# A channel shuffle: loads and stores moved from two DMA queues to one, with 4 MB tiles in place of 2 MB and all copies on VectorE

## The chip, the cores and the metric

The kernel runs on one core of one Trainium2 chip. The metric is the device time of one execution in microseconds, and lower is better. "Span" is the profiled part of an execution.

## The reference

The input is a float32 array of 16 x 64 x 64 pixels with 256 channels, 67.11 MB. The channels of each pixel are seen as 8 groups of 32, and the two axes are swapped.

```python
def reference(x, groups):                      # x: (16, 64, 64, 256), groups: 8
    batch, h, w, c = x.shape
    x = x.reshape(batch, h, w, groups, c // groups)
    x = x.transpose(0, 1, 2, 4, 3)
    return x.reshape(batch, h, w, c).astype(np.float32)
```

There is no arithmetic. Every byte is read once from HBM, moved within its pixel, and written once: 134.22 MB in all.

## The kernel before

Each tile gives each of the 128 partitions 16 whole pixels, 16 KB, which lie together in DRAM. A tile is loaded from SyncE, permuted by one strided copy on GpSimd or VectorE in turn, and stored from ScalarE. Loads and stores therefore stand in two DMA queues, and five buffers on each side let them run ahead.

```python
q = 16                                   # pixels per partition: 16 KB rows, 2 MB tiles, 32 tiles
in_pool = ...tile_pool(name="in_pool", bufs=5)
out_pool = ...tile_pool(name="out_pool", bufs=5)
copy_engines = [nc.gpsimd, nc.vector]
for t in range(ntiles):
    in_tile = in_pool.tile([P, free], mybir.dt.float32)
    nc.sync.dma_start(out=in_tile, in_=x_t[t])
    out_tile = out_pool.tile([P, free], mybir.dt.float32)
    src = in_tile.rearrange("p (i g j) -> p i j g", g=G, j=CPG)
    dst = out_tile.rearrange("p (i j g) -> p i j g", j=CPG, g=G)
    copy_engines[t % 2].tensor_copy(out=dst, in_=src)
    nc.scalar.dma_start(out=out_t[t], in_=out_tile)
# [... views, asserts and the launch are cut ...]
```

Of the kernel before, what the change touches and what calls it, by code (L numbers as in the profile page):

```python
# [2 lines left out]

# [4 lines left out]


_Q = int(os.environ.get("CS_Q", "16"))
_IN_BUFS = int(os.environ.get("CS_IN_BUFS", "5"))
_OUT_BUFS = int(os.environ.get("CS_OUT_BUFS", "5"))
_COPY_ENGINES = os.environ.get("CS_COPY_ENGINES", "gv")


@with_exitstack
def kernel(
    ctx: ExitStack,
    tc: tile.TileContext,  # L20
    x: bass.AP,
    groups: bass.AP,
    out: bass.AP,
):
    nc = tc.nc

    b, h, w, c = x.shape
    G = int(groups)
    CPG = c // G
    assert G * CPG == c, (c, G)  # L30

    P = nc.NUM_PARTITIONS

    n_pix = b * h * w
    assert n_pix % P == 0

    q = _Q
    pix_per_tile = P * q
    ntiles = n_pix // pix_per_tile
    assert ntiles * pix_per_tile == n_pix, (n_pix, pix_per_tile)  # L40

    free = q * c

    x_t = x.rearrange("b h w c -> (b h w c)").rearrange(
        "(t p f) -> t p f", p=P, f=free
    )
    out_t = out.rearrange("b h w c -> (b h w c)").rearrange(
        "(t p f) -> t p f", p=P, f=free
    )

    in_pool = ctx.enter_context(tc.tile_pool(name="in_pool", bufs=_IN_BUFS))
    out_pool = ctx.enter_context(tc.tile_pool(name="out_pool", bufs=_OUT_BUFS))

    eng_map = {"v": nc.vector, "g": nc.gpsimd, "s": nc.scalar}
    copy_engines = [eng_map[ch] for ch in _COPY_ENGINES]

    def do_copy(eng, dst, src):
        if eng is nc.scalar:
            eng.copy(out=dst, in_=src)
        else:  # L60
            eng.tensor_copy(out=dst, in_=src)  # L61

    for t in range(ntiles):
        in_tile = in_pool.tile([P, free], mybir.dt.float32)
        nc.sync.dma_start(out=in_tile, in_=x_t[t])  # L65

        out_tile = out_pool.tile([P, free], mybir.dt.float32)

        src = in_tile.rearrange("p (i g j) -> p i j g", g=G, j=CPG)
        dst = out_tile.rearrange("p (i j g) -> p i j g", j=CPG, g=G)  # L70
        do_copy(copy_engines[t % len(copy_engines)], dst, src)

        nc.scalar.dma_start(out=out_t[t], in_=out_tile)


# [1 line left out]
_INS = ['x', 'groups']  # L77
_OUTS = [((16, 64, 64, 256), 'float32')]
#: Inputs that are plain numbers.
_NUMBERS = {'groups': 8}  # L80


# [26 lines left out]
```

## Time and profile before

| | before |
|---|---|
| time, median | 317.98 us (317.81 to 318.05, 4 runs) |
| span | 316.3 us |
| DMA queues | 2, together 99.5% of the 16 engines' span |
| VectorE / GpSimd busy | 63.8 us / 114.7 us |
| one 16 KB packet, steady part | 611 ns |

The first lines are from the profile page of the kernel before: busy tenths of VectorE (DVE), GpSimd (POOL) and the DMA engines in 40 equal slices of the span, what the DMA moved in each slice, and the queues.

```profile
DVE  0344004040130402204021040310404004040040
POOL 0863350803508044080530806217062260713500
DMA  7999999999999999999999999999999999999997
GB/s 290 431 402 431 431 431 431 431 431 433 431 431 431 431 431 431 431 431 431 431 431 431 431 431 431 431 431 431 431 431 431 431 431 431 431 431 431 433 431 332
...
q1 hardware_dynamic: 4608, 67.11, 50.0%
q10 hardware_dynamic: 4608, 67.11, 49.5%
```

The DMA engines are full from end to end and the copy engines are idle most of the time. This kernel is bound by its transfers.

The next view, windows of the kernel before, gives for chosen stretches (start:end in us) the length, the busy time of VectorE and GpSimd with the number of instructions, the clock, the DMA engines' busy share and GB/s.

```profile
4.00:8.00 4.00, 0.00 (x0) 0.00 (x0) 1.00 1.01 434
16.00:20.00 4.00, 3.19 (x1) 1.68 (x1) 1.00 1.01 381
20.00:24.00 4.00, 0.00 (x0) 4.00 (x1) 1.00 1.00 410
40.00:80.00 40.00, 7.70 (x2) 15.22 (x3) 1.00 1.01 431
304.00:308.00 4.00, 0.00 (x0) 0.00 (x0) 1.00 1.01 434
312.00:314.00 2.00, 0.00 (x0) 0.00 (x0) 1.00 1.03 442
314.00:316.00 2.00, 0.00 (x0) 0.00 (x0) 1.00 0.21 90
316.00:318.00 2.00, 0.00 (x0) 0.00 (x0) 1.00 0.00 0
```

Loads alone (4 to 8 us), loads and stores mixed (40 to 80) and stores alone (304 to 308) run at the same 431 to 434 GB/s. There is one dip where the stores begin.

From the page again: the groups of copies (count, then busy time and mean ns of one, then idle time before them and what ended it), and the DMA issues (count, size, median time from issue to landing).

```profile
L61 POOL COPY out_tile<-in_tile 128x4096 f32<-128x4096 f32 x16 | 114.5, 7157 | 182.3 <-DMA in_tile<-in_x_dram 182.3
L61 DVE COPY out_tile<-in_tile 128x4096 f32<-128x4096 f32 x16 | 63.8, 3985 | 240.0 <-DMA in_tile<-in_x_dram 240.0
...
in_tile<-in_x_dram SPq DMA_DIRECT2D x32, 2048.0 KB, 38.8
out_dram<-out_tile ACTq DMA_DIRECT2D x32, 2048.0 KB, 25.3
```

### The profile page before, as it was taken

Reading aid. Unit: us, or ns where it says so; the run is one execution under the profiler, and the core shown is the slowest. Engines: PE = TensorE matmul, PEld = TensorE weight load, DVE = VectorE, ACT = ScalarE, POOL = GpSimd, SP = SyncE. Lnnn points to the kernel's source line nnn. Section 1 sums busy time; section 2 is a strip of 40 time slices with the busy share of each in tenths; the row PEclk is TensorE's granted clock in tenths of the full one; section 3 lists DMA queues with packets and bytes.
Section 4 is the critical chain, followed back from the end, with each engine's and each line's share of the span. In section 5 each row is a group of like instructions: output and inputs, shape, how many; then the busy total and the mean of one; then the engine's idle time right before and its main releaser. Section 6 shows DMA issues by size and latency. Waiting matters only on the chain.

```text
span 316.3 us, 247 instructions
## 1 busy us (share of the span) xinstructions
DVE 63.8 (20%) x16; POOL 114.7 (36%) x20
## 2 busy tenths in 40 slices
DVE  0344004040130402204021040310404004040040
POOL 0863350803508044080530806217062260713500
DMA  7999999999999999999999999999999999999997
GB/s 290 431 402 431 431 431 431 431 431 433 431 431 431 431 431 431 431 431 431 431 431 431 431 431 431 431 431 431 431 431 431 431 431 431 431 431 431 433 431 332
DMA packets 9216, 134.22 MB, mean 424 GB/s; under 512 B 1024, under 2 KB 1024, under 8 KB 1024
## 3 DMA queue, kind: packets, MB, share of 16 engines
q1 hardware_dynamic: 4608, 67.11, 50.0%
q10 hardware_dynamic: 4608, 67.11, 49.5%
HBM read 67.11 MB, written 67.11 MB: 424 GB/s over the span
## 4 chain that ended last, share of the span: by engine, by line
DMA 94%; DVE 1%; SPq 0%; issue 0%; DVEq 0%
DMA in_tile<-in_x_dram 94%; DVE out_tile L61 1%; SPq L65 0%; DVEq L61 0%
## 5 line engine op out<-in xcount | busy, mean ns | idle before, releaser
L61 POOL COPY out_tile<-in_tile 128x4096 f32<-128x4096 f32 x16 | 114.5, 7157 | 182.3 <-DMA in_tile<-in_x_dram 182.3
L61 DVE COPY out_tile<-in_tile 128x4096 f32<-128x4096 f32 x16 | 63.8, 3985 | 240.0 <-DMA in_tile<-in_x_dram 240.0
L90 POOL MEMSET const-float32-0.0<- 128x1 f32 x1 | 0.1, 99 | 0.2 <-issue 0.2
L90 POOL MEMSET const-bfloat16-1.0<- 128x1 bf16 x1 | 0.1, 103 | 0.0
L90 POOL MEMSET const-uint8-127<- 128x1 uint8 x1 | 0.1, 103 | 0.0
L90 POOL MEMSET const-float32-1.0<- 128x1 f32 x1 | 0.1, 99 | 0.0
## 6 DMA issues: line engine op xcount, KB each, us to landing
in_tile<-in_x_dram SPq DMA_DIRECT2D x32, 2048.0 KB, 38.8
out_dram<-out_tile ACTq DMA_DIRECT2D x32, 2048.0 KB, 25.3
```

What stands on the lines that cost most here:

```text
L61: eng.tensor_copy(out=dst, in_=src)
L90: nc = _bacc.Bacc("TRN2", target_bir_lowering=False, num_devices=1)
```

## The change

The change takes tiles of twice the size (32 KB per partition, 4 MB, 16 tiles), three buffers on each side, and all copies on VectorE in two halves per tile. SyncE issues everything. Three loads go first, and then store t and load t+3 alternate. The intent is fewer, larger transfers, and one queue in which the order of reads and writes is fixed.

```diff
-_Q = 16, _IN_BUFS = 5, _OUT_BUFS = 5, _COPY_ENGINES = "gv"     [four lines, shortened]
+_Q = 32
+_COPY = 16
+_BUFS = 3
 [...]
+    def load(t):
+        in_tile = in_pool.tile([P, _Q * c], F32, name="in_tile")
+        nc.sync.dma_start(out=in_tile, in_=x_t[t])
+        in_tiles[t] = in_tile
-    for t in range(ntiles):
-        in_tile = in_pool.tile([P, free], mybir.dt.float32)
-        nc.sync.dma_start(out=in_tile, in_=x_t[t])
-        [... one copy on GpSimd or VectorE ...]
-        nc.scalar.dma_start(out=out_t[t], in_=out_tile)
+    for t in range(_BUFS):
+        load(t)
+    for t in range(n_tiles):
+        in_tile = in_tiles.pop(t)
+        out_tile = out_pool.tile([P, _Q * c], F32, name="out_tile")
+        for k in range(0, _Q, _COPY):
+            [... src, dst: 16 pixels of the tile ...]
+            nc.vector.tensor_copy(out=dst, in_=src)
+        nc.sync.dma_start(out=out_t[t], in_=out_tile)
+        if t + _BUFS < n_tiles:
+            load(t + _BUFS)
```

More of the change, by code (lines that the diff above doesn't have):

```diff
@@ L2 @@
-import os
 from contextlib import ExitStack
@@ L8 @@
 from concourse._compat import with_exitstack
-_Q = int(os.environ.get("CS_Q", "16"))
-_IN_BUFS = int(os.environ.get("CS_IN_BUFS", "5"))
-_OUT_BUFS = int(os.environ.get("CS_OUT_BUFS", "5"))
-_COPY_ENGINES = os.environ.get("CS_COPY_ENGINES", "gv")
+F32 = mybir.dt.float32
+P = 128
+_Q = 32
+_COPY = 16
+_BUFS = 3
 @with_exitstack
@@ L29 @@
     CPG = c // G
-    assert G * CPG == c, (c, G)
-    P = nc.NUM_PARTITIONS
+    assert G * CPG == c
     n_pix = b * h * w
-    assert n_pix % P == 0
-    q = _Q
-    pix_per_tile = P * q
-    ntiles = n_pix // pix_per_tile
-    assert ntiles * pix_per_tile == n_pix, (n_pix, pix_per_tile)
-    free = q * c
+    n_tiles = n_pix // (P * _Q)
+    assert n_tiles * P * _Q == n_pix
     x_t = x.rearrange("b h w c -> (b h w c)").rearrange(
-        "(t p f) -> t p f", p=P, f=free
+        "(t p f) -> t p f", p=P, f=_Q * c
@@ L46 @@
     )
     out_t = out.rearrange("b h w c -> (b h w c)").rearrange(
-        "(t p f) -> t p f", p=P, f=free
+        "(t p f) -> t p f", p=P, f=_Q * c
     )
-    in_pool = ctx.enter_context(tc.tile_pool(name="in_pool", bufs=_IN_BUFS))
-    out_pool = ctx.enter_context(tc.tile_pool(name="out_pool", bufs=_OUT_BUFS))
-    eng_map = {"v": nc.vector, "g": nc.gpsimd, "s": nc.scalar}
-    copy_engines = [eng_map[ch] for ch in _COPY_ENGINES]
-    def do_copy(eng, dst, src):
-        if eng is nc.scalar:
-            eng.copy(out=dst, in_=src)
-        else:
-            eng.tensor_copy(out=dst, in_=src)
@@ L63 @@
-    for t in range(ntiles):
-        in_tile = in_pool.tile([P, free], mybir.dt.float32)
-        nc.sync.dma_start(out=in_tile, in_=x_t[t])
-        out_tile = out_pool.tile([P, free], mybir.dt.float32)
-        src = in_tile.rearrange("p (i g j) -> p i j g", g=G, j=CPG)
-        dst = out_tile.rearrange("p (i j g) -> p i j g", j=CPG, g=G)
-        do_copy(copy_engines[t % len(copy_engines)], dst, src)
-        nc.scalar.dma_start(out=out_t[t], in_=out_tile)
+    in_pool = ctx.enter_context(tc.tile_pool(name="in_pool", bufs=_BUFS))
@@ new lines @@
+    out_pool = ctx.enter_context(tc.tile_pool(name="out_pool", bufs=_BUFS))
+    in_tiles = {}
+    def load(t):
+        in_tile = in_pool.tile([P, _Q * c], F32, name="in_tile")
+        nc.sync.dma_start(out=in_tile, in_=x_t[t])
+        in_tiles[t] = in_tile
[5 more added lines that the diff above has]
+        for k in range(0, _Q, _COPY):
+            cols = slice(k * c, (k + _COPY) * c)
+            src = in_tile[:, cols].rearrange("p (i g j) -> p i j g", g=G, j=CPG)
+            dst = out_tile[:, cols].rearrange("p (i j g) -> p i j g", j=CPG, g=G)
+            nc.vector.tensor_copy(out=dst, in_=src)
+        nc.sync.dma_start(out=out_t[t], in_=out_tile)
+        if t + _BUFS < n_tiles:
+            load(t + _BUFS)
```

## The prediction

> **What bounds the kernel now.** The 16 DMA engines. The queue table gives 50.0% + 49.5% of their span, and the chain of waits is 94% input load. The windows view gives 434 GB/s at 4-8 us (loads alone), 431 at 40-80 us (both mixed) and 434 at 304-308 us (stores alone), so the rate depends neither on direction nor on the number of queues in use. In the packet records every 16 KB packet of the steady part takes 611 ns: 8192 packets / 16 engines x 0.611 us = 312.8 us of the 316.3 us span. The rest is the start (about 2.7 us until data flows), a dip when the first stores begin (windows view, 16-24 us: 381 and 410 GB/s, about 0.6 us lost), and the last completions. The Trainium skill, "DMA: Bandwidth & Descriptors", section "Where 436 GB/s comes from", states a ceiling of 435.2 GB/s; this trace reaches 431, 99% of it. VectorE is busy 63.8 us (20%), GpSimd 114.7 us (36%).
>
> **What the change removes.** All 16 GpSimd copies (7.11 us each) and ScalarE's store issues. VectorE takes everything: 32 copies of the same 128x4096 shape at 3.86 us (one that overlapped GpSimd took 5.79) = 124 us, 39% of the span, still hidden. DMA issues fall from 64 to 32, each 328-338 ns, off the critical path after the start. The 1024 completion packets of 9 ns become 512: 0.58 us per engine becomes 0.29.
>
> **What it moves.** Stores now stand in the same queue as loads: L0 L1 L2 S0 L3 S1 L4 ... Does the queue run dry? A 4 MB transfer takes about 9.7 us. L0 lands near 12 us, two copies end near 20, S0 and L3 are issued, while L1 and L2 keep the engines busy until about 31 us. In the steady state, when load t lands, S(t-2), L(t+1), S(t-1), L(t+2) are queued behind it: 39 us of work; S(t) follows after 7.8 us. So SyncE's waits have some 31 us of slack. At the end S13 and S14 (19 us) cover the last copy, so the tail stays one completion. The same page, section "Issuing engines are not separate DMA queues", says that queues of different issuers share the 16 engines, so giving up the second queue should cost no bandwidth; the trace agrees as far as it can (434 GB/s with one queue alone).
>
> **What may gain.** A row per partition grows from 16 to 32 KB. If it goes as one packet and part of the 611 ns is fixed per packet (estimate from the 435.2 GB/s ceiling: 16 KB would take 602 ns, so up to 9 ns), the transfer falls by up to 2.2 us. If it is cut into 16 KB packets, or has no fixed part, only about 0.3 us. I take a middle.
>
> **Predicted time.** 317.0 us, range 315.0 to 319.0. Chances: faster by over 2% 0.02, within 2% 0.93, slower by over 2% 0.05.
>
> **What would show it.** Right: 430-434 GB/s in every middle slice; one DMA queue; VectorE about 124 us over 32 copies; load issue to landing grows, because up to 20 MB queue ahead; the chain still DMA. Packets of 32 KB at 1214-1222 ns, or 16 KB at 611.
>
> **What would make it wrong.** The trace never shows one queue switching between loads and stores. If each of about 29 switches lost as much as the first stores' dip (0.6 us), that would be 17 us, 5% slower, visible as middle slices near 405 GB/s with longer packets. A limit on transfers outstanding in one queue would show as gaps between packets.

## The result, and the profile after

The changed kernel takes 321.07 us (320.31 to 321.86, 4 runs) against 317.98 us. The ratio is 1.0096, with a 95% interval of 1.0079 to 1.0113. Ratios here are the mean time of one kernel's fast runs over that of the other's of the same rounds, so they are not quite the ratio of the medians quoted. The change is slower by about 1%, and the time lies outside the predicted range of 315 to 319 us.

The profile page of the changed kernel, the same lines as shown of before:

```profile
DVE  0378813509045090440904408054080631707200
POOL 0000000000000000000000000000000000000000
DMA  8999999999999999999999999999999999999993
GB/s 328 431 423 394 431 423 443 414 447 431 431 431 423 443 431 423 439 419 435 435 431 431 414 447 431 427 435 419 443 439 419 439 410 456 431 419 439 419 451 135
...
q1 hardware_dynamic: 4608, 134.22, 98.2%
```

The DMA engines are still full, and one queue carries everything. The middle slices now scatter between 394 and 456 GB/s, where the prediction wanted 430 to 434 in each, but they average about the same. The last slice stands out: 135 GB/s where it was 332, with the DMA engines at 3 tenths where they had 7.

Windows of the changed kernel, with the same columns:

```profile
4.00:8.00 4.00, 0.00 (x0) 0.00 (x0) 1.00 0.95 410
28.00:30.00 2.00, 2.00 (x1) 0.00 (x0) 1.00 0.97 393
30.00:32.00 2.00, 0.34 (x1) 0.00 (x0) 1.00 1.03 262
40.00:80.00 40.00, 16.02 (x5) 0.00 (x0) 1.00 1.00 432
304.00:308.00 4.00, 0.00 (x0) 0.00 (x0) 1.00 0.95 410
312.00:314.00 2.00, 0.00 (x0) 0.00 (x0) 1.00 0.69 295
314.00:316.00 2.00, 0.00 (x0) 0.00 (x0) 1.00 0.30 131
316.00:318.00 2.00, 0.00 (x0) 0.00 (x0) 1.00 0.11 49
```

At 40 to 80 us the rate is 432 GB/s, no lower than before. From 312 us on it fades to 295, 131 and 49 GB/s over some six microseconds, where the kernel before stopped within two. The work is not slower on the whole: the 16 engines no longer finish together.

The group of copies and the DMA issues of the changed kernel, from its page:

```profile
L60 DVE COPY out_tile<-in_tile 128x4096 f32<-128x4096 f32 x32 | 122.4, 3880 | 175.0 <-DMA in_tile<-in_x_dram 175.0
...
in_tile<-in_x_dram SPq DMA_DIRECT2D x16, 4096.0 KB, 50.9
out_dram<-out_tile SPq DMA_DIRECT2D x16, 4096.0 KB, 41.2
```

VectorE does all 32 copies in 122.4 us and idles 175.0 us waiting for loads, so compute is still hidden. SyncE, however, waits for VectorE. The view of waits of the changed kernel, for the DMA queue's own sequencer (total us, times, longest):

```profile
SPq L61 <- DVE out_tile L60: 282.3, 16, 19.5
```

Those 282.3 us look alarming and cost nothing that shows. The DMA engines have 4 MB transfers queued meanwhile, and no slice between the first and the last falls below 9 tenths. (Run w2, below, takes away nearly all of this wait and is no faster.) A wait counts only if the engine that bounds the kernel runs dry.

**Where the engines part.** The Trainium skill, "DMA: Bandwidth & Descriptors", section "Why a DMA increments its semaphore by 16 and not by 1", says that a DMA over 128 partitions is split over 16 engines, each of which adds one to the semaphore when its part has landed. The trace agrees: it holds 1024 such increments for the 64 DMAs of before, and 512 for the 32 of after. The time from the first to the last of a DMA's 16 increments therefore tells how far the engines have drifted apart. I worked it out from the completion records of each trace. The columns are points at eighths of the DMAs, in order of completion, and the values are us:

```
                          1/8  2/8  3/8  4/8  5/8  6/8  7/8  last
before                    1.8  1.8  1.8  1.8  1.8  1.8  1.8  0.7
changed kernel            0.5  0.7  1.5  2.6  3.3  4.3  4.8  5.1
changed, again (d0)       0.5  0.7  1.2  2.9  3.3  4.4  5.0  5.2
```

In the kernel before, the engines keep a fixed distance and end 0.7 us apart. In the changed kernel, a few engines fall back steadily. At the end the last increment comes 4.6 us after the median one, and the first only 0.5 us before it. Every DMA has one increment from each engine, so the slowest engine sets when it is done, and the last DMA's slowest engine sets the time. No trace here shows an engine doing more than its share to help a late one.

**When they fall back.** The packet records show 32 KB packets of 1213 ns nearly throughout. After 40 us, 78 of the 4096 packets take over 1240 ns, up to 1872. Engines are not named in these records, so packets were chained to engines by their end and start times, with each engine held to 32 DMAs of 8 packets and one completion. Packets that end together can still be swapped. By this order, 76 of the 78 are among the last two packets that an engine does of a load before it turns to a store (78 of 90 in d0, and 50 of 53 in w2, below). Those places hold two of the 16 packets of a load and a store. The extra time is uneven: after 40 us four engines collect 3.4 to 4.1 us of it, two 1.2 and 1.5 us, and the other ten 0.3 us at most.

### The profile page after: what moved, and what is told of

Its sections match the earlier page's. It is cut to its first block, busy times and chain, and to the rows that moved or that the text cites. A ratio compares the mean times of both kernels' runs of the same rounds, so it can differ in the third digit from the quotient of the medians.

```text
span 319.4 us, 133 instructions
## 1 busy us (share of the span) xinstructions
DVE 122.4 (38%) x32; POOL 0.2 (0%) x4
## 4 chain that ended last, share of the span: by engine, by line
another core or an unknown queue 41%; DVE 30%; DMA 20%; DVEq 1%; issue 0%; SPq 0%
DVE out_tile L60 30%; DMA in_tile<-in_x_dram 20%; DVEq L94 1%; DVEq L60 0%; SPq L48 0%; SPq L61 0%
## 5 line engine op out<-in xcount | busy, mean ns | idle before, releaser
L60 DVE COPY out_tile<-in_tile 128x4096 f32<-128x4096 f32 x32 | 122.4, 3880 | 175.0 <-DMA in_tile<-in_x_dram 175.0
## 6 DMA issues: line engine op xcount, KB each, us to landing
in_tile<-in_x_dram SPq DMA_DIRECT2D x16, 4096.0 KB, 50.9
```

The lines of the kernel that those rows point to most:

```text
L60: nc.vector.tensor_copy(out=dst, in_=src)
```

## The experiments

I call a change from a load to a store in one queue's order a turn. The changed kernel has 14 of them (the last two stores follow a store). Theory A: turns in one queue make the engines fall apart, and the larger packets give back a part. Rival B: the 32 KB packets themselves share unevenly. Rival C: late issue, the buffers or VectorE.

All runs gave right results unless said otherwise. They were made in four sittings, each on a chip of its own: e1, e2, e3 and e4; c1, c2, c3 and e3b; the d runs; the w runs. The kernel before took 317.94 to 318.12 us (medians) beside them, so times of two sittings can be compared to about 0.2 us. Diffs are against the changed kernel unless said otherwise.

| run | queues | packets | turns | time, us | ratio to before (95%) | last spread, us |
|---|---|---|---|---|---|---|
| changed kernel | 1 | 32 KB | 14 | 321.07 | 1.0096 (1.0079 to 1.0113) | 5.1 |
| e1 | 2 | 32 KB | - | 323.73 | 1.0178 (1.0163 to 1.0193) | 1.8 |
| e2 | 1 | 16 KB | 27 | 320.91 | 1.0091 (1.0074 to 1.0108) | 3.4 |
| e3 | 1 | 32 KB | 6 | 318.19 | 1.0008 (0.9993 to 1.0023) | 0.6 |
| e4 | 2 | 32 KB | both turn | 324.63 | 1.0216 (1.0178 to 1.0255) | 7.0 |
| c1 | 2 | 16 KB | - | 317.87 | 1.0005 (0.9989 to 1.0021) | 1.3 |
| c2 | 1 | 16 KB | 14 | 321.75 | 1.0114 (1.0099 to 1.0130) | 4.6 |
| c3 | 2 | 16 KB | - | 317.72 | 0.9992 (0.9977 to 1.0007) | 0.4 |
| e3b | 1 | 32 KB | 6 | 319.95 | 1.0062 (1.0045 to 1.0079) | 0.6 |
| d0 (changed, again) | 1 | 32 KB | 14 | 321.39 | 1.0097 (1.0083 to 1.0112) | 5.2 |
| d1 | 1 | 8 KB | 53 | 321.85 | 1.0124 (1.0111 to 1.0137) | 1.8 |
| d2 | 2 | 32 load, 16 store | - | 327.95 (fast runs) | 1.0309 (1.0259 to 1.0359) | 4.9 |
| d3 | 2 | 16 load, 32 store | - | 323.72 | 1.0180 (1.0166 to 1.0193) | 0.2 |
| w1 (wrong result) | 1 | 32 KB | 1 | 316.12 | 0.9941 (0.9927 to 0.9954) | 0.7 |
| w2 (wrong result) | 1 | 32 KB | 14 | 321.25 | 1.0110 (1.0091 to 1.0129) | 4.5 |
| w4 | 1 | 32 KB | 4 | 317.27 | 0.9981 (0.9968 to 0.9994) | 1.2 |

Turns are counted from the order of issue. Two texts below give 29 turns for e2 and 61 for d1; with their six and twelve loads ahead, 27 and 53 are right. The last spread does not tell all: in e1 and d3 the engines part by up to 5.5 and 9.2 us before the end.

### e1: a queue of its own for the stores

```diff
-        nc.sync.dma_start(out=out_t[t], in_=out_tile)
+        nc.scalar.dma_start(out=out_t[t], in_=out_tile)
```

> Only edit against the changed kernel: the stores are issued from ScalarE, so they have a queue of their own; 4 MB tiles, 32 KB packets, three buffers and VectorE copies stay. Theory A (one queue turning from loads to stores costs: packets in flight at each turn are lengthened, unevenly over the engines): beyond the first stores nothing turns any more, so packets over 1240 ns are gone after the first stores' dip, the engines finish within 1 us of each other, and the 2.3 us from the larger packets are kept: 315 to 316.5 us, faster than both kernels (ratio to before 0.992 to 0.996). Rival B (32 KB packets themselves jitter and share unevenly over the engines): 320 to 322 us, still a long tail.

Measured: 323.73 us, a clear miss. With two queues the kernel became slower still. Beyond the first stores, load packets are lengthened about every 20 us, the duration of a 4 MB load and a 4 MB store side by side. Turns inside one queue cannot be the whole story, and 32 KB packets on two queues have a loss of their own. A part of it is waiting at the end: the last store was issued at 308.62 us, after its copies, and from 306.6 to 309.5 us the engines stood idle for 1.4 us on average. The changed kernel has no such gap.

### e2: 2 MB tiles on one queue

```diff
-_Q = 32
+_Q = 16
-_BUFS = 3
+_BUFS = 6
```

> One queue as in the changed kernel, but tiles of 2 MB in six buffers each (same SBUF, same order of loads and stores): 29 turns from loads to stores instead of 14, 16 KB packets of 611 ns as before. Theory A, with a fixed loss per turn: about 5.5 us lost (the changed kernel lost about 3 us to the before kernel and gave back 2.3) become about 10: 323 to 330 us, long packets at every turn. Rival B (packet size): with 16 KB packets back to 318 us. Rival C (single queue loses at its issue waits or at its end only): 320 to 322 us.

Measured: 320.91 us. The loss did not double, against A with a fixed loss per turn, and did not vanish with 16 KB packets, against B. It lies in the range of rival C, which w2 tests below. The spread grows to 3.4 us within the first third and then stays there: 1.0, 2.6, 3.5, 3.4, 3.4, 3.5, 3.5, 3.4 at the eighths. The lag thus stopped growing, here at about 70% of the 4.9 us that one DMA takes (8 packets of 611 ns).

### e3: loads and stores in groups of three

The order in the queue becomes three loads, three stores, and so on (3, 3, 3, 3, 2, 2 tiles).

```diff
-    for t in range(_BUFS):
-        load(t)
-    for t in range(n_tiles):
-        [... copy t, store t ...]
-        if t + _BUFS < n_tiles:
-            load(t + _BUFS)
+    first = 0
+    for size in [3, 3, 3, 3, 2, 2]:
+        these = range(first, first + size)
+        first += size
+        for t in these:
+            load(t)
+        for t in these:
+            copy(t)              # the same two copies, then the store
```

> One queue, 4 MB tiles, but the order is three loads, three stores (3,3,3,3,2,2 tiles): 6 turns from loads to stores instead of 14; everything else as in the changed kernel. The queue should not run dry: with groups of two and more the copies end while other transfers are queued. Theory A: loss shrinks to 5 of 13 turns after the first: 316.5 to 318.5 us. Rival B (packet size): 320 to 322 us, as the changed kernel.

Measured: 318.19 us, as A expected. The spread never exceeds 1 us, and the engines end together. One thing was not foreseen: at 274 us, where a store is followed by a load, all 16 engines lost about 0.9 us at once.

### e4: two queues that turn in opposed phases

```diff
+    queues = [nc.sync, nc.scalar]
-        nc.sync.dma_start(out=in_tile, in_=x_t[t])
+        queues[t % 2].dma_start(out=in_tile, in_=x_t[t])
-        nc.sync.dma_start(out=out_t[t], in_=out_tile)
+        queues[t % 2].dma_start(out=out_t[t], in_=out_tile)
```

> Two queues, but each turns: even tiles load and store on SyncE's queue, odd tiles on ScalarE's, so that each queue turns 6 or 7 times, in opposed phases (while one loads the other stores) and the sum of loads and stores in flight stays mixed. If the turn costs in the queue (A1, each ring pays when it goes from a load to a store): long packets at the turns, loss as with one queue, 319 to 322 us. If it costs because the whole flow turns from reading HBM to writing it (A2): no long packets after the first stores, 315 to 317 us.

Measured: 324.63 us, outside both ranges, with a spread that grows to 7.0 us. The test decides nothing between A1 and A2. Its 32 KB packets stand on two queues, where e1 lost time without any turns in a queue, and the flow was not evenly mixed: in the packet records, 11 or more of the 16 engines were on the same queue at three moments of four, for instance 14 on one queue at 103.0 us and 14 on the other 1.2 us later.

### c1: e2 with two queues

```diff
# against e2
-        nc.sync.dma_start(out=out_t[t], in_=out_tile)
+        nc.scalar.dma_start(out=out_t[t], in_=out_tile)
```

> The kernel e2 (2 MB tiles, six buffers each, VectorE copies) with its stores on ScalarE's queue: one edit from e2, and from the kernel before it differs only in six buffers for five and in VectorE for both copy engines. If the one queue costs what e2 lost: 317.5 to 318.3 us, all engines' completions within 2 us of each other to the end. If VectorE alone or the buffer count were at fault: 320 to 322 us.

Measured: 317.87 us. One word moves the time from 320.91 to 317.87 us. The two ran on different chips, but the kernel before took 317.94 and 318.00 us beside them; c2 and c3 repeat the pair on one chip. VectorE alone and six buffers change nothing against the kernel before, so that part of rival C is out. One queue costs 3.0 us at 2 MB.

### c2: the changed kernel with 16 KB packets

```diff
     x_t = x.rearrange("b h w c -> (b h w c)").rearrange(
-        "(t p f) -> t p f", p=P, f=_Q * c
+        "(t k p f) -> t p k f", k=2, p=P, f=_Q * c // 2
     )                                        # out_t likewise
-        nc.sync.dma_start(out=in_tile, in_=x_t[t])
+        nc.sync.dma_start(out=in_tile.rearrange("p (k f) -> p k f", k=2), in_=x_t[t])
                                              # the store likewise
```

> The changed kernel with the same 4 MB DMAs in the same order, but each partition's row cut into two DRAM pieces of 16 KB, so packets of 16 KB (611 ns expected). If stragglers come from the order of the DMAs (turns of 4 MB in one queue): the spread of the engines' completions still grows to about 5 us, and time is the changed kernel's plus 2.3 us of packet cost, 322 to 324.5 us. If they come from 32 KB packets: the spread stays under 2 us and time is 317.5 to 319.5 us.

Measured: 321.75 us, and the spread grows to 4.6 us (0.7, 1.2, 2.2, 2.7, 3.0, 3.4, 4.1, 4.6). The stragglers do not come from 32 KB packets: rival B is out for one queue. The time is a little under the range given; the drift is a little smaller too.

### c3: e1 with 16 KB packets

This is c2 with its stores on ScalarE.

> The kernel e1 (two queues, 4 MB DMAs, three buffers, 323.7 us) with packets of 16 KB. If e1's loss came from 32 KB packets taking turns on two queues: 317.5 to 319 us. If it came from DMAs of 4 MB with three buffers: 323 to 326 us, the spread growing to about 5 us as in e1.

Measured: 317.72 us, with the spread constant at 1.6 us and 0.4 at the end. The DMA engines' busy tenths, first c2 (one queue), then c3 (two queues):

```profile
DMA  7999999999999999999999999999999999999993
```

```profile
DMA  7999999999999999999999999999999999999997
```

The same DMAs of 4 MB with three buffers are as fast as the kernel before, as soon as the packets are 16 KB. The loss of e1 belongs to 32 KB packets on two queues.

### e3b: other groups

```diff
# against e3 (shortened to the list of groups)
-[3, 3, 3, 3, 2, 2]
+[3, 2, 3, 3, 3, 2]
```

> As e3 (one queue, grouped loads and stores) but groups of 3,2,3,3,3,2 tiles, to see whether e3's second stall of all engines (0.9 us at 274 us, after two pairs in a row) comes again and where. If it belongs to pairs or to the end: a stall after the first pair or near the end, 318 us. If it was chance: one stall only, at the first stores, 316.5 to 317.5 us. The spread of completions should stay under 1.5 us.

Measured: 319.95 us, well over what either case expected. The engines stay within 2.1 us (1.5 was expected) and end 0.6 us apart, but stalls of all engines came at about 100 and 130 us, after the first pair, beside the one at the first stores. The first of the two came at the end of the pair, where a store is followed by a load, just as in e3; the second came one turn later. That speaks for pairs and against chance, but why pairs should do it no run shows. Few turns keep the engines nearer together, but they do not guard against this second loss. The 0.6 us at the end flatters, for the queue also ran dry: the first store of the last pair was issued only at 295.97 us, after its copies, and from 295.5 to 296.9 us up to eleven of the 16 engines stood idle. That let the late ones catch up, so the lag they had by then was lost time all the same.

### d0: the changed kernel again

> The changed kernel again, unedited, beside the next three on one chip: 320.3 to 322 us, and the spread of the engines' completions of one DMA again growing from about 0.6 us to 4 to 6 us. If the spread were an accident of one profile, it would stay under 2 us.

Measured: 321.39 us, with the spread growing to 5.2 us as in the first profile. The drift is a property of the kernel and not of one profile.

### d1: 1 MB tiles on one queue

```diff
-_Q = 32, _COPY = 16, _BUFS = 3
+_Q = 8, _COPY = 8, _BUFS = 12
```

> One queue in the same order, tiles of 1 MB (8 KB packets), twelve buffers each: 61 turns, but only 2.4 us of loads between turns. With 602 ns per 16 KB and 9 ns per packet fixed, as 611 and 1213 ns say, an 8 KB packet takes 310 ns and the transfer grows by 4.6 us over 16 KB packets. Stragglers: in e2 (2 MB) the spread stopped growing at 3.4 us, 70% of one DMA; if a straggler can lag no more than part of one DMA, it stops near 1.7 us here: 322.5 to 325 us in all. If every turn cost the same with no such bound, 61 turns would give a spread over 6 us and 328 us or more.

Measured: 321.85 us, 0.65 us under the range. An 8 KB packet takes 309 ns (expected 310), and the spread creeps up to 1.8 us (expected 1.7). The lag is smaller with the smaller DMA, but the transfer is longer: 1024 packets of 309 ns are 316.4 us for an engine, where e2's 512 of 611 ns are 312.8.

### d2 and d3: unequal packets on two queues

```diff
# d2: the store in two halves, on ScalarE (d3: the load in two halves on SyncE, the store whole on ScalarE)
-        nc.sync.dma_start(out=out_t[t], in_=out_tile)
+        for half in (slice(0, _Q * c // 2), slice(_Q * c // 2, _Q * c)):
+            nc.scalar.dma_start(out=out_t[t][:, half], in_=out_tile[:, half])
```

> Two queues; loads of 4 MB in 32 KB packets from SyncE, stores from ScalarE as two halves of 2 MB in 16 KB packets. Theory (a loss comes only where loads run alone on all engines and stores then begin): loads run ahead of stores two to one, wait for buffers, and the stores always have a backlog, so after the first stores nothing is lost and half of the packet gain is kept: 316.3 to 317.3 us, faster than both. If any 32 KB packet on two queues costs as in e1 (323.7): half or all of its loss, 320 to 324 us.

> The mirror: loads as two halves in 16 KB packets, stores of 4 MB in 32 KB packets on ScalarE's queue. Stores drain two to one, so their queue runs empty, loads run alone and each store begins anew: by the theory long packets at every store, 319 to 324 us, clearly over d2. If only packet size mattered, it equals d2.

Measured: d2 327.95 us in its four fast runs (325.62, 325.91, 329.99 and 330.09; two more, of 331.30 and 331.98 us, count as slow, being over 1.5% above the fastest, and with them the median is 330.04), d3 323.72 us. d2 is a miss by over 10 us, and it refutes the reason that I gave for it, that only loads alone followed by stores lose. The loads did run ahead as expected: in the trace they land 20.4 us after issue and the stores 48.9 us. The load queue then ran dry and stores ran alone for 4 to 5 us in every 20, and when the loads came back, packets of both kinds were lengthened. d3 lay in its range and under d2, not over it; its last store came late too, and the engines stood idle for about 1.9 us on average near 309 us. None of the three with 32 KB packets for loads or stores on two queues (e1, d2, d3) was as fast as the same with 16 KB for both (c3).

### w1 and w2: one turn against fourteen

Both give a wrong result, so that the order of the DMAs is free of the data. The copies of tiles 0 and 1 go to two tiles that every store sends, and all other copies go to a scratch tile.

```diff
+    out_tiles = [out_pool.tile([P, _Q * c], F32, name=f"out_tile{i}") for i in "ab"]
+    scratch = out_pool.tile([P, _Q * c], F32, name="scratch")
+    # load_and_copy(t): load t, two copies to out_tiles[t] if t < 2 else scratch
+    # store(t): nc.sync.dma_start(out=out_t[t], in_=out_tiles[t % 2])
+    for t in range(n_tiles):          # w1: all loads, then all stores
+        load_and_copy(t)
+    for t in range(n_tiles):
+        store(t)
# w2: the changed kernel's order
+    for t in range(n_tiles + 2):
+        if t < n_tiles:
+            load_and_copy(t)
+        if t >= 2:
+            store(t - 2)
```

> Wrong result on purpose. One queue, the same 16 loads and 16 stores of 4 MB in 32 KB packets and the same 32 copies as the changed kernel, but all loads first and then all stores (which send tiles 0 and 1 again and again): one turn from loads to stores. If the turns make the stragglers: the spread of one DMA's completions stays under 1 us and the time is 315.3 to 316.8 us (256 packets of 1213 ns per engine are 310.5 us, about 2.6 us start, about 0.9 us at the one turn, 1.7 us between span and time). If one long queue lets engines drift apart by itself: spread over 3 us, 319 to 322 us.

> Wrong result on purpose, and the control of w1: the same kernel with the DMAs in the changed kernel's order (14 turns from loads to stores); the stores hardly wait for copies, since they send tiles 0 and 1 again. If the turns make the stragglers: the spread grows to 4 to 6 us, 320 to 322 us. If the loss came from the stores' waiting for copies (late issue): as w1.

Measured: w1 316.12 us, w2 321.25 us. Windows of w1, columns as above:

```profile
312.00:314.00 2.00, 0.00 (x0) 0.00 (x0) 1.00 0.04 16
314.00:316.00 2.00, 0.00 (x0) 0.00 (x0) 1.00 0.00 0
```

Windows of w2:

```profile
312.00:314.00 2.00, 0.00 (x0) 0.00 (x0) 1.00 0.38 164
314.00:316.00 2.00, 0.00 (x0) 0.00 (x0) 1.00 0.27 115
316.00:318.00 2.00, 0.00 (x0) 0.00 (x0) 1.00 0.04 16
```

w1 is over by 312 us, while w2 fades out as the changed kernel does. The spreads at the eighths:

```
w1 (1 turn)     0.8  0.8  0.8  0.7  0.7  0.7  0.7  0.7
w2 (14 turns)   0.4  0.4  1.6  2.8  3.2  4.1  4.5  4.5
```

w2's stores hardly wait for VectorE (the queue's waits of w2, the two on copies):

```profile
SPq L58 <- DVE out_tilea L55: 18.7, 1, 18.7
SPq L58 <- DVE out_tileb L55: 8.9, 1, 8.9
```

Both have the same queue, the same packets, the same bytes and the same number of copies. The order is worth 5.1 us, and the drift comes and goes with it. About 0.8 us of the 5.1 is not drift but the dip at the first stores, where long packets cost an engine 0.84 us on average in w2 and 0.02 us at the turn of w1. A long single queue does not drift by itself (w1), and waiting for copies is not the cause either: 27.6 us of such waits are left in w2, of the 282.3 in the changed kernel, and it still drifts. Two things change along with the order: in w1 the copies all fall in the half with the loads, and loads are issued less far ahead (they land 21.4 us after issue, in w2 51.1). Neither looks like the cause. In c1 and c3 copies run beside stores to the end and the engines stay together, and in d1 loads land 19.7 us after issue and the engines part, though by less. But neither was changed alone.

w1 holds a surprise. Its one turn shows almost no loss: only two packets were lengthened there (beyond the start, no others were), while the first stores of every other kernel were dearer (the changed kernel: 262 GB/s at 30 to 32 us). A turn does not cost a fixed amount.

### w4: four loads, four stores, in place

```diff
+    slots = [pool.tile([P, _Q * c], F32, name=f"slot{i}") for i in range(5)]
+    for first in range(0, n_tiles, 4):
+        for i in range(4):
+            nc.sync.dma_start(out=slots[i + 1], in_=x_t[first + i])
+        for i in range(4):
+            [... two copies from slots[i + 1] to slots[i] ...]
+            nc.sync.dma_start(out=out_t[first + i], in_=slots[i])
```

> A right version meant to keep the packet gain on one queue: five slots of 4 MB; four loads into slots 1 to 4, each copied into the slot before it, four stores from slots 0 to 3, and so on: 4 turns from loads to stores (e3 had 6, the changed kernel 14). By the theory spread under 1.5 us; 316.5 to 318 us, at or a little under the kernel before; if whole-engine stalls of 0.9 us come at further turns, as twice in e3 and thrice in e3b, 318 to 319 us.

Measured: 317.27 us (316.89 to 318.27, 5 runs), ratio 0.9981 (0.9968 to 0.9994). This is the lowest time of a right version, but only 0.2% under the kernel before, and the interval of c3's ratio overlaps its own; that it beats c3 is not shown. It did clear the changed kernel, by over 1% in the ratios. The engines stay within 1.2 us, and a stall of about 1 us came at the first stores only.

## Why the prediction was wrong, point by point

- **What bounds the kernel.** Right. The transfers do, before and after.
- **Copies and issues stay hidden.** Right. VectorE took 122.4 us (124 predicted), and c1 shows that VectorE alone costs nothing.
- **The queue does not run dry.** Right. No slice between the first and the last falls below 9 tenths, the packet records show no gap before the end, and loads land 50.9 us after issue.
- **"giving up the second queue should cost no bandwidth".** This is the step that failed. The evidence named for it, 434 GB/s with one queue alone, came from stretches in which that queue only loaded or only stored. In its place the runs show that alternating loads and stores in one queue lengthens the last packets of a load before a store, on a few engines more than on others. In alternation the order costs 5.1 us (w2 against w1, wrong results both), and one queue for two costs 3.0 us at 2 MB (e2 against c1) and 4.0 us at 4 MB with 16 KB packets (c2 against c3). At the changed kernel's own 32 KB packets, a second queue would not have saved it: e1 is 2.7 us slower still, by another loss.
- **"the tail stays one completion".** Wrong, and this is where the loss shows. The last DMA's engines end 5.1 us apart, 0.7 before.
- **What may gain.** The mechanism was right, and the size was at the upper end of what was named. A 32 KB packet takes 1213 ns, so the engine needs 256 x 1.213 = 310.5 us where it needed 512 x 0.611 = 312.8. That is 2.3 us; the prediction took a middle of 0.3 and 2.2. Without the turns the gain is there: w1 is 1.9 us faster than before. With -1.9 for w1 and +5.1 for the order, one is at w2, +3.3; the changed kernel, whose stores do wait for their copies, lost 3.1.
- **What would make it wrong.** The switch between loads and stores was named as the risk, but its form was not: it was taken as a lower rate in all middle slices, equal for all engines, 17 us in all. Measured after 40 us, long packets cost an engine 1.2 us on average, and middle windows still read 430 to 433 GB/s. The loss lies in its unevenness, since six of the 16 engines collect most of it.
- **The chain still DMA.** The page does not show it so. The chain that ended last, by engine, in the kernel before and then in the changed kernel:

```profile
DMA 94%; DVE 1%; SPq 0%; issue 0%; DVEq 0%
```

```profile
another core or an unknown queue 41%; DVE 30%; DMA 20%; DVEq 1%; issue 0%; SPq 0%
```

The second line puts 41% to an unknown queue and 30% to VectorE, which idled 175.0 us for loads and cannot be the limit. The windows and the completions tell more here than the chain.

**What stays open.** Why a turn lengthens the packets in flight, why some engines are hit again and again, and why some turns (w1's, most of e3's) are free is not shown by any run. The same goes for the 0.9 us stalls after pairs and for the reason why 32 KB packets lose on two queues and 16 KB packets do not. That a late engine is hit because it is late, so that the lag feeds itself up to a bound, fits the growth in the changed kernel and the levels that e2 and d1 reach, but it was not tested by itself. Each run keeps one trace, so how far the drift varies between executions is known for the changed kernel alone (two traces).

## What to carry to other kernels

When transfers bound a kernel, look at whether the engines finish together, and not only at how busy they are: here a few microseconds of drift in a few of them were the time of all. For a stream like this one, of equal loads and stores, try two queues with packets of 16 KB, as c1 and c3 do, or, on one queue, long runs of each direction as w4 does; e3b shows that not every grouping pays. A rate measured in one direction did not tell the rate of a queue that alternates.

## What the Trainium skill lacked or had wrong

- "DMA: Bandwidth & Descriptors", sections "Issuing engines are not separate DMA queues" and "Rules for kernel authors": spreading DMAs over issuing engines is said only to save the sequencer's issue time. Here the same DMAs took 320.91 us from one engine and 317.87 us from two (e2, c1), with the issue time hidden in both. With 32 KB packets it was the other way round: 321.07 us from one and 323.73 us from two (the changed kernel, e1).
- The same page's "Rules for kernel authors" give, for the most bandwidth, 128 partitions and at least 1 MiB per DMA. All runs here keep to that, and the packet mattered beside it: on two queues, 4 MB DMAs took 317.72 us in 16 KB packets and 323.73 us in 32 KB packets (c3, e1). That larger packets can lose, the page does not have.
- No page that I read has that the 16 engines drift apart when one queue alternates loads and stores: up to 5.2 us here (d0), against 0.8 us at most with one turn (w1). The order was worth 5.1 us (w2 against w1).
- Nothing is wrong with the ceiling in its section "Where 436 GB/s comes from", on which the prediction's estimate rests: 16 packets of 32 KB in 1213 ns are 432 GB/s, under its ceiling of 435.2.
